# Hybrid encoder block: v column first over eight banks, both halves of the output projection in one bank, first left operands formed earlier

## Chip, core and metric

The kernel runs on one core of one Trainium2 chip. The metric is the device time of one execution in microseconds. PE is the matrix engine, DVE the vector engine, ACT the scalar engine, POOL the general engine, SP the engine that issues most DMAs.

## The reference

x has 2048 rows of 1024. One input projection to 5 x 512 columns gives q, k, v (8 heads of 64) and u, vg (gated group). Attention is stick-breaking and strictly causal; the gated part mixes positions in blocks of 128. Both are normalized, concatenated and projected back; then follows an MLP with squared ReLU (1024 to 4096 to 1024) and a last norm.

```python
    h = rmsnorm(x, norm_mix_g)
    q, k, v, u, vg = split(h @ w_in)
    a_out = stick_breaking_attention(q, k, v)
    b_out = gelu(u) * (W_s layernorm(gelu(vg)) + b_s)      # per block of 128 rows
    a_out = rmsnorm(a_out, out_norm_g[:512]); b_out = rmsnorm(b_out, out_norm_g[512:])
    x = x + concat(a_out, b_out) @ w_out
    x = x + square(relu(rmsnorm(x, norm_mlp_g) @ w_up)) @ w_down
    return rmsnorm(x, norm_final_g)
```

## The kernel before

Everything is fp32. Each matmul operand is split into a high part (ACT copy, L81 or L84) and a low part (DVE subtraction, L82 or L85), and `mm3` (L89 to L91) makes three matmuls of them: high x high, high x low, low x high. A bank of PSUM takes 512 columns.

The 2048 rows are four chunks of 512. The program runs in this order.

1. `proj([0, 1])`: input projection of chunks 0 and 1 together, five columns of 512. `weight` loads a quarter of a column into a staging tile `st` (three of them in all, shared with `operand`, which loads x transposed, and `norms`, which loads x for the row norms), splits it, and stores the halves to `wi_d` for chunks 2 and 3. `natural` makes 24 matmuls for one bank (a row block of 128 x 512 columns, both parts of eight k blocks), then calls the evacuation: `evac_vg` (gelu, LayerNorm), `evac_u` (gelu, and for each pair of row blocks the mixing matmuls at L244 and the product with u), `evac_v` (split and store). The order of columns is vg, u, k, q, v. `gelu` takes an ACT copy and square, a DVE scalar op (L213), a DVE product (L214), a sigmoid and a last product.
2. `proj([2])` and `proj([3])`, with the attention of earlier chunks between their matmuls. An attention step (`weigh`, `gather`) makes a score tile z for 128 queries and up to 512 keys on PE, a running product on DVE (the scans L331 and L334, the product L335), four transposes on PE (L345), a split of them (aT at L81 and L82) and two matmuls with v (L363, L364).
3. For each chunk an `Out`: `operands` loads a (attention, transposed) and b (gated), splits them and transposes b; `product` makes the output projection in groups of four row blocks: for each of two halves of 512 columns first b's part, then a's part, each in a bank of its own, each evacuated by one DVE operation at L509 that scales by the row norm and adds to x; `turn` norms the result and transposes it for the MLP. The first two Outs stand before `up_plain` (chunks 0 and 1), the third before `down_plain`, the fourth beside it.
4. `up_plain` and `down_plain` are the MLP of chunks 0 and 1 in the plain way, with attention beside them. `up_seven` and `down_seven` are the MLP of chunks 2 and 3 by a seven-product scheme: `Rights` forms sums of the activation tiles (`minus`, L668) and keeps seven of them split (`keep`), and each of 16 turns forms seven sums of weights (by POOL) and splits them (w0 to w6). All of `rest` stands within the first turn, after the last plain output.

`together` interleaves such generators at fixed ratios when the program is written; the building layer then sets the order on each engine. Tiles of 8 KB per partition (`t8`, 14 of them in one pool for Outs and plain MLP; the fourth Out has eight of its own) are handed on by slots: a load into a slot waits until its last reader is done. All loads except the stores to `wi_d` and some outputs are issued by SP, in order.

## Time and profile before

| | us |
|---|---|
| median of 3 runs (lowest, highest) | 2577.95 (2577.49, 2582.44) |
| the profiled execution | 2578.94 |
| its span on the core | 2577.2 |
| PE busy | 2435.4 |
| DVE busy | 1719.5 |
| ACT busy | 1154.8 |
| POOL busy | 321.3 |

The profiled execution is 1.0 above the median and has 1.7 outside its span. Matmuls overlap in their records, so start to start is their price, not their length. A wait names the instruction that was released and the one that released it. The windows give the mean granted clock of TensorE (1.00 is the upper of its levels of 2.4 and 1.2 GHz).

### The profile page before, as it was taken

The numbers are of one execution on the slowest core, as the hardware profiler recorded it, in microseconds if no ns is written. First come the engines' busy times: TensorE is split into PE (matmuls) and PEld (weight loads), VectorE is DVE, ScalarE is ACT, GpSimd is POOL, SyncE is SP. The second block draws the span as 40 slices with busy tenths as digits, with TensorE's granted clock in tenths as the row PEclk, the third lists the DMA queues.
The fourth block names the chain that finished last, engine by engine and source line by source line (L and its number), as shares of the span: only waits on it lengthen the run. The fifth ranks groups of instructions, "written<-read, shape, count | busy, mean of one in ns | idle before, by whom it ended". The sixth has DMA issues, their size and how long they took to land.

```text
span 2577.2 us, 30195 instructions
## 1 busy us (share of the span) xinstructions
PE 2435.4 (94%) x11328; PEld 1974.1 (77%) x11328; DVE 1719.5 (67%) x2312; ACT 1154.8 (45%) x2004; POOL 321.3 (12%) x263
## 2 busy tenths in 40 slices
PE   7799989998979999999989799999979999999997
PEld 5688767786757888888778688888767888778886
DVE  4733359877787666666676788744557665677787
ACT  5323236546454555555563544422135455433333
POOL 1100001101010000000010000010023222223331
PEclk9899999999989999999999999999999999999999
DMA  7378787678764344343355733255233434663422
GB/s 269 148 253 262 250 258 228 205 216 256 264 221 152 113 125 119 123 123 115 123 178 175 248 115 119 86 229 212 98 115 117 159 144 151 231 232 144 161 98 98
DMA packets 153714, 446.59 MB, mean 173 GB/s; under 512 B 12384, under 2 KB 28768, under 8 KB 134368
## 3 DMA queue, kind: packets, MB, share of 16 engines
q1 hardware_dynamic: 145232, 417.39, 48.5%
q0 software_dynamic: 4032, 25.17, 2.4%
q10 hardware_dynamic: 4304, 2.10, 0.3%
q8 instruction: 90, 1.47, 0.2%
q14 instruction: 56, 0.46, 0.1%
HBM read 314.59 MB, written 130.02 MB: 173 GB/s over the span
## 4 chain that ended last, share of the span: by engine, by line
PE 76%; DVE 14%; DMA 4%; ACT 2%; issue 2%; POOL 1%; SPq 0%; DVEq 0%; POOLq 0%; ACTq 0%
PE mm L90 21%; PE mm L91 21%; PE mm L89 21%; PE tr L345 3%; PE av L363 2%; PE av L364 2%; DVE w L82 2%; PE z L321 2%; PE z L320 2%; DVE pr L334 2%; DVE pr L331 2%; DVE aT L82 1%; DVE b L332 1%; DMA w_in<-wi_d 1%; DVE t L82 1%
## 5 line engine op out<-in xcount | busy, mean ns | idle before, releaser
L91 PE MATMUL mm<-t,t 128*128 128x512 f32 x1280 | 501.4, 392 | 0.0
L90 PE MATMUL mm<-t,t 128*128 128x512 f32 x1280 | 500.8, 391 | 0.0
L89 PE MATMUL mm<-t,t 128*128 128x512 f32 x1280 | 497.4, 392 | 2.6 <-DVE t L639 2.5
L326 ACT ACTIVATE kk<-z 128x512 f32<-128x512 f32 (+2 forms) x320 | 171.2, 535 | 382.2 <-PE z L321 262.9
L334 DVE TENSOR_TENSOR_SCAN pr<-kk,pr,zeros 128x513 f32<-128x513 f32 x192 | 248.7, 1295 | 118.0 <-ACT kk L326 117.6
L89 PEld LDWEIGHTS mm<-t,t 128*128 128x128 f32 x1280 | 240.5, 188 | 53.9 <-DVE t L639 2.9
L91 PEld LDWEIGHTS mm<-t,t 128*128 128x128 f32 x1280 | 240.7, 188 | 51.5
L90 PEld LDWEIGHTS mm<-t,t 128*128 128x128 f32 x1280 | 240.5, 188 | 50.7 <-DVE t L82 0.4
L345 PE MATMUL tr<-ident,b 128*128 128x128 f32 x1088 | 185.3, 283 | 40.8 <-DVE aT L82 28.6
L82 DVE TENSOR_TENSOR aT<-tr,aT 128x512 fp32r<-128x512 f32 (+1 forms) x320 | 191.2, 599 | 32.7 <-ACT aT L81 32.4
L81 ACT ACTIVATE aT<-tr 128x512 fp32r<-128x512 f32 (+1 forms) x320 | 173.0, 542 | 81.9 <-PE tr L345 80.4
L345 PEld LDWEIGHTS tr<-ident,b 128*128 128x128 f32 x1088 | 133.8, 144 | 87.2 <-DVE aT L82 38.8
L90 PE MATMUL mm<-w,w 128*128 128x512 f32 x448 | 177.0, 395 | 10.4 <-DVE w L82 8.8
L91 PE MATMUL mm<-w,w 128*128 128x512 f32 x448 | 175.9, 393 | 0.0
L89 PE MATMUL mm<-w,w 128*128 128x512 f32 x448 | 172.8, 391 | 0.2 <-ACT w L81 0.2
L81 ACT ACTIVATE t<-t 128x1024 fp32r<-128x1024 f32 x104 | 105.5, 1064 | 147.4 <-DMA t<-in_w_down 73.1
L328 ACT ACTIVATE b<-z 128x512 f32<-128x512 f32 (+2 forms) x320 | 170.8, 534 | 1.0 <-PE tr L345 1.0
L82 DVE TENSOR_TENSOR w<-raw,w 128x512 fp32r<-128x512 f32 (+1 forms) x136 | 155.9, 1149 | 13.3 <-ACT w L81 12.8
L331 DVE TENSOR_TENSOR_SCAN pr<-kk,zeros 128x128 f32<-128x128 f32 (+3 forms) x128 | 107.8, 844 | 79.8 <-ACT kk L326 79.2
L81 ACT ACTIVATE w<-raw 128x512 fp32r<-128x512 f32 (+1 forms) x136 | 107.2, 800 | 113.0 <-PE mm L91 98.2
L363 PE MATMUL av<-aT,vt 128*128 128x512 f32 (+1 forms) x320 | 142.6, 446 | 8.0 <-DVE ao L373 4.4
L82 DVE TENSOR_TENSOR t<-t,t 128x1024 fp32r<-128x1024 f32 x104 | 124.5, 1218 | 26.9 <-PE mm L90 15.0
(200 smaller groups left out, 4786.1 us busy)
## 6 DMA issues: line engine op xcount, KB each, us to landing
w_in<-wi_d SPq DMA_DIRECT2D x40, 1024.0 KB, 7.7
kt<-k_d SPq DMA_DIRECT2D x160, 256.0 KB, 4.8
s_d<-acts SPq DMA_DIRECT2D x16, 1792.0 KB, 6.2
raw<-s_d SPq DMA_DIRECT2D x28, 1024.0 KB, 4.8
t<-wo_d SPq DMA_DIRECT2D x24, 1024.0 KB, 8.4
wi_d<-w_in POOLq DMA_DIRECT2D x20, 1024.0 KB, 9.9
vt<-v_d SPq DMA_DIRECT2D x80, 256.0 KB, 2.8
t<-in_w_up SPq DMA_DIRECT2D x16, 1024.0 KB, 7.7
```

Source lines behind the costliest of these rows:

```text
L81: nc.scalar.activation(hi, src, AF.Copy)
L82: nc.vector.tensor_tensor(lo, src, hi.bitcast(F32), ALU.subtract)
L89: nc.tensor.matmul(ps, lh, rh, start=first, stop=False, skip_group_check=more)
L90: nc.tensor.matmul(ps, lh, rl, start=False, stop=False, skip_group_check=more)
L91: nc.tensor.matmul(ps, ll, rh, start=False, stop=last, skip_group_check=more)
L320: nc.tensor.matmul(z[:, :Z], ql, kt[:, 0, :Z], start=True, stop=False)
L326: nc.scalar.activation(kk[:, :L], z[:, :L], AF.Sigmoid, scale=-QK_SCALE)
L328: nc.scalar.activation(b[:, :L], z[:, :L], AF.Sigmoid, scale=QK_SCALE)
L331: nc.vector.tensor_tensor_scan(pr[:, L - 1::-1], kk[:, L - 1::-1], zeros[:, :L], 1.0, ALU.mult, ALU.add)
L334: nc.vector.tensor_tensor_scan(pr[:, ::-1], kk[:, ::-1], zeros, carry[tb], ALU.mult, ALU.add)
L345: nc.tensor.transpose(tr[:, tb * P:(tb + 1) * P], bs[tb][:, j * P:(j + 1) * P], ident)
L363: nc.tensor.matmul(av[:, t0:], vt[:, j, :], aT[:, 0, t0:], start=first, stop=False)
```

## The change

1. Start. The first column of `proj([0, 1])` is v, by `first_col`: eight banks open at once, the quarters of k outside, so that each quarter of the weights and operands feeds 48 matmuls. Staging tiles are seven of their own. The norms come after all operands. The columns then go vg, u, k, q.
2. `gelu`: the square carries the constant, and one DVE operation takes the place of two.
3. `Out`: b is scaled (by its row norm over a's) before its transposes, so that both parts of a half run into one bank, and one evacuation does for both: 8 instead of 16 in an Out. The row norms of a and b, with their small matmul, move into `operands`. All four weight tiles of a half are wanted before its first bank ends.
4. The raw weights and the first sums come from one set of nine tiles; `Lefts` forms w0 and w4 of the first turn beside `down_plain`; hc[4] is kept after the last plain output instead of before. In `down_seven` the weights are loaded in tiles of 8 KB instead of 16, and y and acc lie in such tiles.

```diff
+        col0 = 2 if cs[0] == 0 else 4 if gated_first else 1
...
+        def first_col(col, evac):
+            ws = weights(col)
+            banks = [[places[ci].ps() if (ci, tb) != (0, 3) else places[1].ps() for tb in range(NTB)]
+                     for ci in range(2)]
+            for k2 in range(KD // 2):
+                for ci, (c, pl) in enumerate(zip(cs, places)):
+                    for tb in range(NTB):
+                        ts_ = slice(tb * P, (tb + 1) * P)
+                        w, h = ws[k2], hT[ci][k2]
+                        for j in range(2):
+                            mm3(banks[ci][tb], h[:, 0, j, ts_], h[:, 1, j, ts_], w[:, 0, j, :], w[:, 1, j, :],
+                                k2 == 0 and j == 0, k2 == KD // 2 - 1 and j == 1)
+                        if k2 == KD // 2 - 1:
+                            evac(pl, c * TC + tb * P, ci * NTB + tb, banks[ci][tb])
+                        yield
...
-            nc.scalar.activation(t, dst, AF.Square)
-            nc.vector.tensor_scalar(t, t, GELU_A, 1.0, ALU.mult, ALU.add)
-            nc.vector.tensor_tensor(t, t, dst, ALU.mult)
+            nc.scalar.activation(t, dst, AF.Square, scale=GELU_A ** 0.5)
+            nc.vector.scalar_tensor_tensor(t, t, 1.0, dst, ALU.add, ALU.mult)
...
             for k2 in range(KD // 2):
-                if c == 0:
-                    ready[col0].append(weight(col0, k2))
-                hT[i].append(operand(c, pl, k2))
-            norms(c, pl)
-        if cs[0] == 0:
+                ready[col0].append(weight(col0, k2))
+                for i, (c, pl) in enumerate(zip(cs, places)):
+                    hT[i].append(operand(c, pl, k2))
+            for c, pl in zip(cs, places):
+                norms(c, pl)
             gates_ready()
+            yield from first_col(col0, evac_v)
...
+            nc.gpsimd.tensor_tensor(rb, rb, root, ALU.mult)
+            self.ras = [ra[:, tb:tb + 1] for tb in range(NTB)]
+            yield
             bm = self.bm = rm.pair([4, TC])
             for tb in range(NTB):
...
+                nc.scalar.activation(st[:, tb, :], st[:, tb, :], AF.Copy, scale=rb[:, tb:tb + 1])
                 ps = rm.ps((P, 4, P))
...
-            yield from group(0, 1, self.bm, self.rbs)
...
-            yield from group(1, 0, self.am, ras)
+            for half in range(2):
+                ws = [self.weights(half, part) for part in range(2)]
...
+                    for part, m in ((0, self.am), (1, self.bm)):
+                        for e in range(4):
+                            mm3(ps, m[0][:, e, ts_], m[1][:, e, ts_], ws[part][0][:, e, :], ws[part][1][:, e, :],
+                                part == 0 and e == 0, part == 1 and e == 3)
...
+                    nc.vector.scalar_tensor_tensor(ys[tb][:, hs], ps, self.ras[tb], ys[tb][:, hs], ALU.mult, ALU.add)
...
-            self.keep(4, b11, bigs)
...
             if step == 0:
-                self.keep(5, self.t2, bigs)
-                self.keep(1, self.b21, bigs)
+                self.keep(4, self.b11)
+                self.keep(5, self.t2)
+                self.keep(1, self.b21)
...
-    bufs = dict(bigx=2, w8=5, big=5, raw8=2, acts=2, t2=3)
-    rm = Room(None, None, bufs, dict(bigx=hx, w8=hx))
-    rights = Rights(lambda *a: rm.get("bigx", *a), lambda *a: rm.get("w8", *a))
+    rm = Room(None, None, dict(w8=9, s12=1, t8=12, acts=2, t2=2), dict(w8=hx, s12=hx))
+    rights = Rights(rm)
+    ahead = Lefts(rm, 0)
     together(down)
```

How this moves instructions, at four places. First the loads that SP issues at the start. Before, x (for the norms) stands between the operands of the two chunks, and the weights of the second column behind all of it:

```order
L121 DMA st<-in_w_in 128x1024
L135 DMA st<-in_x_t 128x1024
L145 DMA st<-in_x 128x1024 x4
L135 DMA st<-in_x_t 128x1024 x4
L145 DMA st<-in_x 128x1024 x4
L121 DMA st<-in_w_in 128x1024 x8
```

and now, from the last quarter of the operands on; the five weight tiles behind the gates are the four of vg and the first of u:

```order
L124 DMA stx<-in_w_in 128x1024
L138 DMA stx<-in_x_t 128x1024 x2
L148 DMA stx<-in_x 128x1024 x8
L942 DMA ln_g_t<-in_ln_g 128x512
L943 DMA ln_b_t<-in_ln_b 128x512
L944 DMA sgw_t<-in_sgw 128x1024
L946 DMA sgb_t<-in_sgb 128x8
L947 DMA outg_t<-in_outg 128x8
L124 DMA stx<-in_w_in 128x1024 x5
L226 DMA v_d<-qkv_st 128x8x128
```

All operands now stand ahead of x, and the stores of v alternate with weight loads from here on.

Second, PE where the first mixing stands (L244 before, L263 now; hT and hTx are the operands of chunks 0 and 1). Before, right behind the vg column, with a few matmuls of u around it:

```order
L91 MATMUL mm<-w_in,hTx 128x512
L89 MATMUL mm<-w_in,hT 128x512 x2
L244 MATMUL mm<-vn,sgw_t 128x128 x4
L89 MATMUL mm<-w_in,hTx 128x512 x2
L244 MATMUL mm<-vnx,sgw_t 128x128 x6
L90 MATMUL mm<-w_in,hT 128x512
```

and now behind two whole banks of u:

```order
L89 MATMUL mm<-w_in,hT 128x512
L90 MATMUL mm<-w_in,hT 128x512
L91 MATMUL mm<-w_in,hT 128x512
L263 MATMUL mm<-vn,sgw_t 128x128 x8
L89 MATMUL mm<-w_in,hT 128x512
L90 MATMUL mm<-w_in,hT 128x512
```

The mixing moved behind 48 matmuls. Third, PE inside the second Out's product (in mm<-t8,t8 the first tile is of the weights, the second of a or b; z, tr and av are of attention). Before, where the last group's weights (t8_6632, t8_6633) take over from the one before, one score tile is issued:

```order
L90 MATMUL mm_6596<-t8_6492,t8_6082 128x512
L91 MATMUL mm_6596<-t8_6491,t8_6083 128x512
L320 MATMUL z_6615<-kt_6610,qt_6316 128x512
L321 MATMUL z_6615<-kt_6610,qt_6316 128x512
L345 MATMUL tr_6624<-ident_60,b_6438 128x128
L363 MATMUL av_6593<-aT_6555,vt_6314 128x384
L364 MATMUL av_6593<-aT_6555,vt_6314 128x384
L89 MATMUL mm_6636<-t8_6632,t8_6180 128x512
L90 MATMUL mm_6636<-t8_6633,t8_6180 128x512
```

and now, where the second half's weights begin (t8_6438 is their first tile), three banks are begun with that one tile, and attention goes on before the next tile (t8_6439) is used:

```order
L370 MATMUL tr_6756<-ident_60,b_6598 128x128
L89 MATMUL mm_6446<-t8_6438,t8_6035 128x512
L89 MATMUL mm_6513<-t8_6438,t8_6035 128x512
L89 MATMUL mm_6581<-t8_6438,t8_6035 128x512
L370 MATMUL tr_6756<-ident_60,b_6631 128x128
L388 MATMUL av_6510<-aT_6681,vt_6385 128x512
L389 MATMUL av_6510<-aT_6681,vt_6385 128x512
L345 MATMUL z_6788<-kt_6659,qt_6664 128x512
L346 MATMUL z_6788<-kt_6659,qt_6664 128x512
L348 LDWEIGHTS ident_b_65
```

Two score tiles, z_6788 and the next, stand between the first and the second weight tile of that half, and one (z_6746) just before. Counted over the order of PE, score tiles z issued up to a place are:

| place on PE | before | now |
|---|---|---|
| last input projection ends | 78 | 78 |
| first Out: product begins, ends | 92, 98 | 96, 98 |
| second Out: product begins, ends | 116, 121 | 120, 125 |
| up_plain begins | 128 | 129 |
| third Out: operands begin | 250 | 251 |
| third Out: product begins, ends | 260, 267 | 256, 268 |
| down_plain begins | 276 | 280 |

Last DVE at the start of the seven products, from the last plain output on (w_15029 to w_15032 are Rights' sums, big the kept halves, nf the last norm). Before:

```order
L73 TENSOR_SCALAR nf_m<-nf_ssq 128x1
L648 SCALAR_TENSOR_TENSOR t_12270<-t_12270,nf_r,gfin_t 128x1024
L82 TENSOR_TENSOR big<-w_15029,big 128x1024 x2
L82 TENSOR_TENSOR big<-w_15031,big 128x1024 x2
L668 TENSOR_TENSOR w_15031<-w_15031,w_15029 128x1024
L82 TENSOR_TENSOR w_15948<-raw_15943,w_15948 128x512
L82 TENSOR_TENSOR w_15948<-t_15945,w_15948 128x512
L668 TENSOR_TENSOR w_15031<-w_15031,w_15029 128x1024
L82 TENSOR_TENSOR big<-w_15030,big 128x1024 x2
L82 TENSOR_TENSOR w_15967<-t_15945,w_15967 128x512
```

and now (w_14886 to w_14890 are Rights' sums, the t tiles the kept halves, s_14909 and w_14907 the sums of weights):

```order
L73 TENSOR_SCALAR nf_m<-nf_ssq 128x1
L673 SCALAR_TENSOR_TENSOR t_12185<-t_12185,nf_r,gfin_t 128x1024
L82 TENSOR_TENSOR t_15821<-w_14886,t_15820 128x1024 x2
L82 TENSOR_TENSOR t_15827<-w_14887,t_15826 128x1024 x2
L82 TENSOR_TENSOR t_15833<-w_14889,t_15832 128x1024 x2
L693 TENSOR_TENSOR w_14889<-w_14889,w_14887 128x1024 x2
L82 TENSOR_TENSOR w_15841<-s_14909,w_15841 128x512
L82 TENSOR_TENSOR w_15841<-w_14907,w_15841 128x512
L82 TENSOR_TENSOR t_15848<-w_14888,t_15847 128x1024 x2
L82 TENSOR_TENSOR w_15853<-w_14907,w_15853 128x512 x2
```

A third pair of kept halves (t_15821, hc[4]) moved to the front of this piece, and w0 and w4 have left it.

## Rows read from the trace of the kernel before

**Rows 1.** The page: busy time of an engine (share of span), and the chain by engine.

```profile
PE 2435.4 (94%) x11328; PEld 1974.1 (77%) x11328; DVE 1719.5 (67%) x2312; ACT 1154.8 (45%) x2004; POOL 321.3 (12%) x263
...
PE 76%; DVE 14%; DMA 4%; ACT 2%; issue 2%; POOL 1%; SPq 0%; DVEq 0%; POOLq 0%; ACTq 0%
```

**Rows 2.** Windows: busy us of PE, PEld, DVE, ACT, POOL (count), clock, DMA share, GB/s.

```profile
17.00:27.00 10.00, 6.83 (x23) 5.39 (x24) 5.28 (x6) 4.07 (x6) 1.06 (x2) 0.83 0.96 335
66.00:79.40 13.40, 0.22 (x2) 0.11 (x1) 12.96 (x30) 3.54 (x6) 3.10 (x3) 0.59 0.00 0
177.00:221.00 44.00, 44.00 (x193) 35.84 (x192) 15.50 (x20) 9.26 (x12) 2.12 (x4) 1.00 0.73 238
221.00:265.10 44.10, 44.10 (x196) 36.35 (x195) 15.02 (x24) 16.11 (x27) 4.25 (x11) 1.00 1.01 338
```

**Rows 3.** PE's waits from 0 to 131 us: in total, times, longest.

```profile
PE mm L244 <- DVE vnx L231: 13.2, 1, 13.2
PE mm L89 <- ACT hT L84: 11.0, 2, 7.2
PE mm L244 <- DVE ln_m L73: 1.7, 1, 1.7
```

**Rows 4.** DVE's lines from 79.4 to 131.2 us: busy us, mean ns.

```profile
L214 DVE TENSOR_TENSOR gelu_t<-gelu_t,u 128x512 f32<-128x512 f32 x7 | 4.8, 689 | 0.2
L213 DVE TENSOR_SCALAR gelu_t<-gelu_t 128x512 f32<-128x512 f32 x8 | 3.4, 426 | 11.5 <-ACT gelu_t L212 11.5
```

**Rows 5.** Transfers from 0 to 60 us: GB/s in 40 slices of 1.5 us.

```profile
GB/s 0 173 382 276 370 395 401 448 415 407 421 433 372 230 366 437 366 178 421 410 399 341 205 249 229 197 262 254 142 265 254 232 317 287 249 202 205 341 38 0
```

**Rows 6.** Windows of the first two Outs, and behind the third.

```profile
613.60:654.00 40.40, 30.06 (x142) 21.28 (x141) 38.13 (x60) 30.08 (x64) 7.63 (x8) 0.83 0.83 261
654.00:702.00 48.00, 48.00 (x222) 39.59 (x221) 32.11 (x47) 15.87 (x31) 2.11 (x3) 1.00 0.75 279
721.00:756.00 35.00, 24.43 (x105) 17.51 (x104) 33.69 (x47) 23.82 (x47) 8.27 (x6) 0.76 0.75 270
1416.00:1452.00 36.00, 22.82 (x120) 15.59 (x119) 28.47 (x39) 22.84 (x43) 1.48 (x3) 0.91 0.93 303
```

**Rows 7.** DVE's lines from 654 to 721 us.

```profile
L334 DVE TENSOR_TENSOR_SCAN pr<-kk,pr,zeros 128x513 f32<-128x513 f32 x7 | 8.9, 1278 | 0.3 <-ACT kk L326 0.3
L509 DVE SCALAR_TENSOR_TENSOR t<-mm,ra_r,t 128x512 f32<-128x512 f32 x8 | 6.0, 749 | 10.6 <-PE mm L91 10.6
...
L82 DVE TENSOR_TENSOR aT<-tr,aT 128x512 fp32r<-128x512 f32 (+1 forms) x6 | 3.6, 604 | 0.0
```

**Rows 8.** The page's DMA issues: KB each, median us to landing.

```profile
t<-wo_d SPq DMA_DIRECT2D x24, 1024.0 KB, 8.4
```

**Rows 9.** PE's waits from 1334 to 1452 us.

```profile
PE z L320 <- DMA kt<-k_d: 5.3, 1, 5.3
```

**Rows 10.** Timeline of DVE from 1917.5 us: start, us, instruction.

```profile
1923.22 6.78 DVE L82 TENSOR_TENSOR big<-w,big 128x1024 fp32r<-128x1024 f32 x4
1929.92 1.21 DVE L668 TENSOR_TENSOR w<-w,w 128x1024 f32<-128x1024 f32 x1
...
1933.39 4.54 DVE L82 TENSOR_TENSOR big<-w,big 128x1024 fp32r<-128x1024 f32 x2
...
1940.27 6.82 DVE L82 TENSOR_TENSOR big<-w,big 128x1024 fp32r<-128x1024 f32 x4
```

**Rows 11.** Timeline of POOL in the same stretch.

```profile
1923.59 0.57 POOL L649 DMA_DIRECT2D out_y<-t  x1 [1.61 <-DVE t L648]
1924.19 1.38 POOL L714 TENSOR_TENSOR t<-raw 128x512 f32<-128x512 f32 x1
1925.64 2.13 POOL L720 TENSOR_TENSOR raw<-raw 128x512 f32<-128x512 f32 x1
```

**Rows 12.** The window from 1918 to 1957 us.

```profile
1918.00:1957.00 39.00, 24.02 (x86) 18.67 (x87) 34.55 (x34) 22.08 (x32) 17.47 (x13) 0.78 0.28 94
```

**Rows 13.** DMA issues from 1917 to 1935 us.

```profile
out_y<-t POOLq DMA_DIRECT2D x3, 512.0 KB, 5.4
```

232 lines of the change are left out of this document (119 added, 113 removed).

## Prediction

> **What bounds the kernel now.** I read the page's first part and its chain first [rows 1]: PE is busy 94% of the span and stands for 76% of the chain that ended last, DVE for 14%. So PE sets the end, and what can be won lies where PE waits. A stretch without waits gives its price: 193 matmuls of 512 columns in 44.00 us, 0.228 us each [rows 2]. By that price I looked for the places where PE does less, by windows and by its waits. There are three, and they are the places that the change touches.
>
> First, the start. Until 131 us PE waits for DVE's vnx 13.2 us in one piece, for the first operand halves (hT) 11.0 us in two pieces of which 7.2 is the wait for the very first, and 1.7 for the LayerNorm [rows 3]. The stretch of the long wait has 0.22 us of PE work and 12.96 of DVE in 13.4 us, at a granted clock of 0.59 [rows 2]: DVE is behind with the gated column, and PE falls to the lower of its two levels meanwhile. Second, the attention around each Out: in 613.60 to 654.00 and 721.00 to 756.00 DVE is full (38.13 of 40.40; 33.69 of 35.00) and PE has 30.06 and 24.43; inside the products it is the reverse (PE 48.00 of 48.00, DVE 32.11) [rows 6]. Third, the start of the seven-product up-projection, 1918 to 1957: PE 24.02, DVE 34.55 of 39.00, at a granted clock of 0.78 [rows 12].
>
> **Part 1: v first, seven staging tiles.** The five columns are 5 x 192 matmuls x 0.228 = 218.9 us. The mixing (64 matmuls of 128 columns) and 8 or 9 small ones are between a quarter of that price and all of it each: 4 to 16 us, and since such matmuls are a quarter as wide I take 8. Sum 227. The fifth column ends at 265.1 [rows 2], so 38 us are lost; three rows of waits hold 25.9 of it [rows 3], the lower clock and short waits are the rest. What stays: 7.2 us before the first operand, some 2 at the lower clock behind it (17 to 27 us has 0.83 [rows 2]). What goes: the 3.8 us second wait, since eight open banks give PE 48 matmuls, 10.9 us, on each weight and operand pair, where before one staging tile had to come free for each; and the 13.2 and 1.7 us, since the gated column now starts with all norms done, its DVE chain runs beside it bank by bank, and two u banks stand ahead of the first mixing.
>
> What comes late next is DVE and the weights. A gated bank's evacuation is one STT for 0.75, one product 0.69 [rows 4], statistics that read 512 elements too, two STTs 1.5 and some small ones, about 4 to 5.5 us, against 24 x 0.228 = 5.47 of PE: level, so little is queued at the end, and two u banks (10.9 us) hide it. The weights: before the last v matmul, at about 7.2 + 43.8 + 2 = 53 us, some 16 MB must have moved (12 tiles of 0.52 MB, 8 of x, 4 MB of stored halves, the gates, the first gated tile). The first 60 us of before, in forty slices, ran at 366 to 448 GB/s in most slices of the first 30 us, where loads were queued, and at 142 to 341 behind them [rows 5]: 16 MB takes 36 to 44 us at the first, up to 60 at about 270. So 0 to 7 us may be lost here; I take 2, nearer the queued rate, since seven staging tiles keep loads queued. The stage ends at 227 + 9 + 2 = 238 to 239: **26 us won**, 19 to 29 as bounds. I count 25, as the v stores now share SP with the u weights: eight of them alternate with weight loads, and each waits for its evacuation. Behind them stand the u weights only, which are wanted 44 us later.
>
> **Part 2: gelu.** One STT (0.75, as [rows 7]) for a scalar op and a product (0.43 and 0.69 [rows 4]): 0.37 us of DVE less, 32 times, 12 us. Where PE is the bound it is worth nothing; the 16 in chunks 2 and 3 lie beside attention, where PE waits now and then. Bounds 0 and 6, **2 taken**. ACT's work is the same.
>
> **Part 3: one bank for both halves.** Eight of the 16 evacuations of an Out go, 8 x 0.75 = 6 us of DVE [rows 7], but inside the product, where PE is the bound: nothing there. Four ACT copies and a POOL chain of small operations come in ahead of b's transposes, beside attention, in a stretch where DVE is the bound: nothing either, or up to 3 us per Out if the transposes come late. What matters is where attention steps stand, by the counts of the table above. A step costs DVE a scan 1.28, a product 0.69 and a subtraction 0.60, 2.57 us [rows 4, 7]; on PE four matmuls of 512 columns, 0.91, and four transposes between a quarter and a whole of that, 1.1 to 1.8, 1.4 taken. In the first two Outs 5 to 8 more steps (three stand around the half boundary) run without product work, and 4 to 7 fewer under it: 5 x 2.57 - 4 x 1.4 - 1.4 = 5.8, or 8 x 2.57 - 7 x 1.4 - 1.4 = 9.4 us lost, the last 1.4 being one step more done by the time of the up-projection. In the third Out 5 more run under the product, 2 fewer outside, and 4 more are done before the plain down-projection: 5 x 1.4 - 2 x 2.57 - 4 x 1.4 = -3.7. Together **4 lost**. The fourth Out lies beside down_plain, where PE has work: nothing. The weights of the second half, 4 MB, can be loaded only when slots come free; a weight tile lands after 8.4 us [rows 8], and the steps at the boundary, 3 x 2.57 = 7.7, cover about that. With both ends: 8 us won if the boundary and the moved steps cost nothing and the evacuations freed DVE for attention, 20 lost if the boundary is bare.
>
> **Part 4: the left operands beside the second product.** Now DVE needs ten 1024-wide subtractions between the last plain output and the first full set; they take 18.1 us with four subtractions of 512 and two differences between them, 6.78 for the first four, 1.7 each, and 1.21 for one by itself [rows 10]. After: w0, w4 and hc0 are done earlier, but keep(4) is moved behind the last output: its tiles lie in the memory of the plain product's pool. Twelve subtractions remain, and keep(5) and keep(1) in part wait until the last out_y store has landed; it is issued at 1923.59 [rows 11] and such stores land 5.4 us later [rows 13], which is 11 us behind PE's last plain matmul (1918). From there by DVE's order: ten more subtractions at 1.2 to 1.8, 12 to 18 us, one difference of two such pieces 2.4, five of 512 3.4, and the last two products of PE behind that: PE ends its first turn 33 to 39 us after the plain product, against 39 now (1918 to 1957 [rows 12]). **3 us won**, 0 to 6.
>
> The Trainium skill speaks against this part: "SBUF — State Buffer" (section on the ports) says that VectorE with two SBUF inputs and a GpSimd operation that reads SBUF take a shared port by turns, and the other waits whole. The trace agrees in kind: the four that took 1.7 us each lie over two POOL additions of 1.38 and 2.13 us [rows 10, 11]. By that rule one addition less in the tight stretch gives 1.4 us back there and takes it beside down_plain, where DVE has room; the sum would be lower by 1.
>
> **Sum.** 2578.94 (the profiled run; 2577.2 span and 1.7 outside) - 25 - 2 + 4 - 3 = 2552.9. The median of the runs is 1.0 under the profiled run: 2552 is the forecast, 2545 to 2560 its own range. The seven-product loops and their end are PE-bound before and after, with deeper prefetch of raw weights: 0, give or take 3.
>
> **The rivals.** (a) The moved steps cost nothing and DVE's saved 12 + 24 us reach the attention stretches: 2552 - 4 - 8 = 2540. For it: DVE is full there [rows 6]. Against: the savings lie in products. (b) The start is limited by transfer at 270 GB/s and the first two boundaries are half bare: 2552 + 5 + 2 x 6 = 2569. For it: rates of 142 to 341 from 35 us on [rows 5]. Against: those were times with three staging tiles. (c) Slower: the second half's weights, 4 MB, at the 303 GB/s that such a stretch reaches [rows 6] take 14 us, and SP issues in order: key tiles of attention queued behind them come late, as the one wait of 5.3 us shows that they can [rows 9]. Then neither PE nor DVE has work: 14 + 5 = 19 us, in the second Out, the fourth (eight slots) and, by its slots, the first: 2552 - 4 + 57 = 2605. It decides against the change when each costs over 10 us. Against: the scheduler put steps at the boundary, and the first Out has slots for part of the weights. (d) The change doesn't do what it says: the gated column still ends with DVE behind, PE waits for its mixing as now, and only the 3.8 us go: 2552 + 15 = 2567, inside (b)'s price.
>
> **Chances.** Forecast 0.50; (a) 0.13; (b) and (d) together 0.22; within 0.2% (5 us, about what a measurement of this kernel can tell from no change) 0.05; (c) 0.10. So faster 0.85, same 0.05, slower 0.10. The range 2541 to 2571 leaves out (c), most of the even case and the tail of (a).
>
> **What would show it.** PE's wait for vnx gone and the five columns done at 236 to 242 us; a wait for w_in at 50 to 60 us would be the weights. Windows of the first two Outs: product stretches of 44 to 47 us with DVE nearly idle, attention stretches longer by 6 to 9 us together. A wait of the product on a DMA t<-wo_d would be (c). First turn of up_seven 33 to 37 us long. The forecast is wrong if attention behind the projection slows (q now ends last, just ahead of its use) or if the boundaries show bare waits.

## The result, and the profile after

The changed kernel takes 2621.15 us (median of 4; 2620.27 to 2626.71), the kernel before, on the same chip, 2580.19 (2577.49 to 2583.14): a ratio of 1.0163, with an interval of 1.0143 to 1.0183. It is 41 us slower, where 26 us faster was forecast, and the time lies beyond the range. The profiled executions have spans of 2618.6 and 2577.2 us.

The page of the changed kernel, busy time by engine (to be read beside [rows 1]):

```profile
PE 2454.1 (94%) x11328; PEld 1985.7 (76%) x11328; DVE 1684.6 (64%) x2236; ACT 1158.5 (44%) x2020; POOL 315.4 (12%) x259
```

DVE does 35 us less, as the diff says. PE has the same 11328 matmuls but is busy 18.7 us longer: the mean granted clock of the execution is 0.972 instead of 0.979, and behind a wait matmuls start further apart (0.43 us behind the one that ends at 2292.49, elsewhere 0.23). The other 22.7 of the 41.4 us are idle time of PE. A share of 94% shows neither. So I cut both traces at the ends of PE's stages (first or last matmul of each, from the traces; us):

| stretch | before | after | difference | forecast |
|---|---|---|---|---|
| start to the end of the five columns | 265.1 | 252.5 | -12.6 | -25 |
| to the end of chunk 3's projection, beside attention | 348.6 | 357.5 | +8.9 | -2 |
| first two Outs, to up_plain | 211.9 | 226.6 | +14.7 | +6 to +9 |
| up_plain | 509.0 | 506.7 | -2.2 | 0 |
| third Out | 117.3 | 120.2 | +2.9 | -4 |
| down_plain with the fourth Out | 465.8 | 471.7 | +5.9 | 0 |
| up_seven (its first turn 39.1, then 38.4) | 327.5 | 327.5 | 0 | -3 |
| down_seven | 322.3 | 344.6 | +22.3 | 0 |
| behind PE's last matmul | 9.8 | 11.2 | +1.4 | 0 |

Half of what was lost lies in down_seven, a stage that the forecast set at nothing. I take four places in order of time.

**The start.** PE's waits from 0 to 131 us in the changed kernel (in total, times, longest; beside [rows 3]):

```profile
PE mm L89 <- ACT hT L84: 7.2, 1, 7.2
PE mm L89 <- ACT vn L231: 3.7, 1, 3.7
PE mm L90 <- DVE w_in L82: 2.8, 1, 2.8
PE mm L89 <- ACT w_in L81: 1.8, 1, 1.8
PE mm L89 <- DVE qkv_st L85: 0.8, 1, 0.8
```

The waits for vnx, ln_m and the second operand are gone, as forecast. New ones have come. Windows of it (busy us of PE, PEld, DVE, ACT, POOL, then clock, DMA share, GB/s):

```profile
0.00:60.00 60.00, 52.80 (x222) 43.38 (x223) 23.41 (x36) 30.26 (x43) 10.60 (x27) 1.00 0.97 379
53.00:64.00 11.00, 11.00 (x50) 9.01 (x48) 0.00 (x0) 0.42 (x1) 0.22 (x1) 1.00 1.00 356
64.00:83.00 19.00, 14.47 (x52) 11.19 (x51) 8.79 (x14) 8.86 (x13) 1.46 (x2) 0.82 1.03 341
105.00:123.00 18.00, 13.41 (x56) 10.58 (x55) 15.86 (x27) 10.48 (x15) 5.56 (x7) 0.91 0.60 225
```

The transfers are full from the first microseconds to 83 us; before, the mean of the 40 slices of the first 60 us was 289 [rows 5]. From 53 to 64 us DVE does nothing at all and ACT 0.42 us, although v's eight banks stand finished (v's last matmul starts at 53.03). ACT's timeline tells why (start, us, instruction, in brackets the idle time before it and what ended it):

```profile
63.58 0.69 ACT L84 ACTIVATE qkv_st<-mm,x_r 128x512 fp32r<-128x512 f32 x1 [12.98 <-DMA v_d<-qkv_st]
...
73.24 0.69 ACT L84 ACTIVATE qkv_st<-mm,x_r 128x512 fp32r<-128x512 f32 x1 [3.10 <-DMA v_d<-qkv_st]
73.83 0.68 ACT L231 ACTIVATE vn<-mm,x_r 128x512 f32<-128x512 f32 x1
```

v's evacuations have two buffers, qkv_st; the third waits 12.98 us until the first store of v has landed behind everything else that is queued. The gated column's first evacuation (73.83) stands behind v's in ACT's order, and PE waits for it.

**The Outs.** Windows of the first two in the changed kernel (attention stretch, product; twice), beside [rows 6]:

```profile
610.00:657.50 47.50, 32.69 (x158) 24.03 (x158) 42.49 (x64) 37.41 (x78) 7.94 (x8) 0.82 0.80 245
657.50:704.00 46.50, 46.50 (x206) 38.33 (x205) 21.46 (x34) 11.76 (x22) 1.12 (x2) 0.97 0.75 281
725.00:771.70 46.70, 31.65 (x138) 22.14 (x137) 38.99 (x54) 30.52 (x61) 8.08 (x7) 0.78 0.74 242
771.70:824.00 52.30, 50.95 (x240) 41.34 (x240) 23.38 (x35) 10.59 (x23) 1.12 (x2) 1.00 0.41 146
```

The stretch from the projection's end to the first product grew from 39.6 us (613.6 to 653.2; the window of [rows 6] ends 0.8 later) to 47.5. From the end of the first product to the start of the second it was 54.1 (701.1 to 755.3) and is 67.8 (704.0 to 771.7). The products themselves went from 47.9 to 46.5 and from 51.1 to 52.2: next to nothing is given back there. Behind the second product, up to up_plain, 19.2 us became 12.7: 6.5 of the 21 us lost up to there come back.

**First turn of up_seven** (beside [rows 12]):

```profile
1935.30:1973.70 38.40, 25.96 (x86) 18.73 (x86) 29.84 (x36) 22.41 (x32) 15.26 (x10) 0.82 0.23 83
```

DVE's work in it fell from 34.55 to 29.84 us, PE's time by 0.7 only.

**down_seven.** The first 40 us of it in the kernel before, then its start in the changed kernel in windows, and below them SP's issues (start, us) from 2250 us on:

```profile
2245.00:2285.00 40.00, 36.12 (x149) 28.40 (x148) 34.76 (x29) 13.45 (x15) 20.63 (x7) 0.96 0.91 357
```

```profile
2268.00:2278.00 10.00, 5.63 (x16) 4.16 (x15) 5.25 (x4) 0.00 (x0) 7.50 (x4) 0.68 0.66 239
2278.00:2288.00 10.00, 2.95 (x12) 2.03 (x11) 2.77 (x4) 0.00 (x0) 2.55 (x2) 0.84 1.02 409
2288.00:2298.00 10.00, 5.51 (x13) 4.03 (x14) 6.48 (x6) 7.57 (x8) 0.00 (x0) 0.50 0.31 129
```

```profile
2250.15 6.90 SPq L808 DMA_DIRECT2D t<-in_w_down  x3
2257.11 2.25 SPq L819 DMA_DIRECT2D t<-y_d  x1
2272.19 0.37 SPq L587 DMA_DIRECT2D s_d<-acts  x1
2272.64 2.99 SPq L819 DMA_DIRECT2D t<-y_d  x3
2275.68 2.13 SPq L857 DMA_DIRECT2D w<-s_d  x2
```

In the changed kernel PE has 14.1 us of work in these 30. The twelve t8 tiles hold six of the seven right operands until up_seven's last turn has formed its products, so the weights of w_down, the four tiles of y, and the operands of the first turns are all wanted in one stretch; and SP, in order, issues the four y loads ahead of w<-s_d. What waited for that, from 2263 to 2303:

```profile
ACT w L81 <- DMA w<-s_d: 23.8, 1, 23.8
...
PE mm L89 <- ACT w L81: 11.5, 1, 11.5
...
PE mm L90 <- DVE w L82: 4.4, 1, 4.4
```

Of the 22.3 us some 15 go here (counted by PE's matmuls, the 192nd of down_seven starts 15.3 us later than before) and 7 near the end of the loop, where PE waits 7.3 us in one piece for DVE's w.

### The profile page after: what moved, and what is told of

It reads as the page before. It is cut to its first block, busy times and chain, and to the rows that moved or that the text cites. A ratio compares the mean times of both kernels' runs of the same rounds, so it can differ in the third digit from the quotient of the medians.

```text
span 2618.6 us, 30138 instructions
## 1 busy us (share of the span) xinstructions
PE 2454.1 (94%) x11328; PEld 1985.7 (76%) x11328; DVE 1684.6 (64%) x2236; ACT 1158.5 (44%) x2020; POOL 315.4 (12%) x259
## 5 line engine op out<-in xcount | busy, mean ns | idle before, releaser
L359 DVE TENSOR_TENSOR_SCAN pr<-kk,pr,zeros 128x513 f32<-128x513 f32 x192 | 248.3, 1293 | 117.3 <-ACT kk L351 116.9
L81 ACT ACTIVATE w<-w 128x512 fp32r<-128x512 f32 (+1 forms) x150 | 121.1, 825 | 299.6 <-DMA w<-s_d 172.3
L82 DVE TENSOR_TENSOR w<-w,w 128x512 fp32r<-128x512 f32 (+1 forms) x150 | 176.5, 1191 | 88.7 <-ACT w L81 86.8
L90 PE MATMUL mm<-w,w 128*128 128x512 f32 x512 | 204.1, 399 | 17.3 <-DVE w L82 17.3
L89 PE MATMUL mm<-w,w 128*128 128x512 f32 x512 | 201.4, 396 | 12.4 <-ACT w L81 11.5
L91 PE MATMUL mm<-w,w 128*128 128x512 f32 x512 | 202.8, 396 | 0.0
L89 PE MATMUL mm<-t,w 128*128 128x512 f32 x384 | 154.0, 401 | 8.9 <-DVE acts L775 4.7
```

Source lines behind the costliest of these rows:

```text
L81: nc.scalar.activation(hi, src, AF.Copy)
L82: nc.vector.tensor_tensor(lo, src, hi.bitcast(F32), ALU.subtract)
L89: nc.tensor.matmul(ps, lh, rh, start=first, stop=False, skip_group_check=more)
L90: nc.tensor.matmul(ps, lh, rl, start=False, stop=False, skip_group_check=more)
L91: nc.tensor.matmul(ps, ll, rh, start=False, stop=last, skip_group_check=more)
L359: nc.vector.tensor_tensor_scan(pr[:, ::-1], kk[:, ::-1], zeros, carry[tb], ALU.mult, ALU.add)
```

## The experiments

Twelve kernels, each beside runs of the kernel before on the same chip. Columns: where the fifth column ends; the stretch from there to the end of chunk 3's projection; the first two Outs; down_seven (us, from the trace of each).

| kernel | median us | ratio (interval) | columns | projections | Outs | down_seven |
|---|---|---|---|---|---|---|
| before | 2580 | | 265.1 | 348.6 | 211.9 | 322.3 |
| after | 2621.15 | 1.0163 (1.0143 to 1.0183) | 252.5 | 357.5 | 226.6 | 344.6 |
| b_start | 2574.99 | 0.9974 (0.9964 to 0.9984) | 257.0 | 352.1 | 212.7 | 321.8 |
| b_out | 2599.74 | 1.0073 (1.0057 to 1.0090) | 265.6 | 349.4 | 228.6 | 321.6 |
| b_tail | 2607.32 | 1.0096 (1.0077 to 1.0115) | 265.5 | 353.6 | 211.4 | 345.5 |
| b_gelu | 2580.47 | 0.9998 (0.9988 to 1.0009) | 264.6 | 353.6 | 211.3 | 320.1 |
| b_sg | 2574.13 | 0.9974 (0.9962 to 0.9987) | 253.3 | 358.6 | 209.9 | 321.9 |
| a_qy | 2615.72 | 1.0133 (1.0118 to 1.0149) | 255.3 | 357.2 | 227.3 | 337.4 |
| b_start_nov | 2559.58 | 0.9919 (0.9904 to 0.9935) | 247.5 | 350.2 | 210.7 | 318.8 |
| b_nov_g0w6 | 2559.77 | 0.9926 (0.9906 to 0.9946) | 247.3 | 356.8 | 209.8 | 321.7 |
| b_nov_pair | 2561.36 | 0.9926 (0.9910 to 0.9943) | 250.7 | 349.8 | 210.6 | 318.4 |
| b_out_nodep | 2591.06 | 1.0037 (1.0017 to 1.0057) | 266.0 | 350.8 | 215.7 | 318.3 |
| b_tail_yt | 2597.19 | 1.0065 (1.0041 to 1.0089) | 265.0 | 350.4 | 211.2 | 337.1 |
| b_tail_own | 2585.95 | 1.0024 (1.0010 to 1.0037) | 265.1 | 352.9 | 210.8 | 326.4 |

**The parts alone.** b_start takes over the hunks of proj (v first, the staging tiles) but for the merged gelu:

```diff
-        col0 = 4 if gated_first else 1
+        col0 = 2 if cs[0] == 0 else 4 if gated_first else 1
+            yield from first_col(col0, evac_v)
```

> The kernel before with the start alone: v first over eight banks and seven staging tiles; gelu, Out and the seven-product part as before. In the changed kernel the fifth column ended at 252.5 us instead of 265.1, and the projections of chunks 2 and 3 then gave back 9 us up to their end (610.0 against 613.6). Theory (two buffers: the stores of v take 14 us to land while loads keep the transfers full, and the third evacuation of v waits for a qkv_st tile): the fifth column ends at 252 to 254 again and PE loses 14 us between 64 and 125 us. If the 9 us given back come from the start (q last, loads of chunk 2 elsewhere), the chunk 3 projection ends at 608 to 611 and the whole is 0 to 4 us faster than before; if they come from gelu, it ends at 600 to 602 and the whole is 11 to 13 us faster.

b_out takes over Out.operands and Out.product:

```diff
-            yield from group(0, 1, self.bm, self.rbs)
+            for half in range(2):
+                ws = [self.weights(half, part) for part in range(2)]
```

> The kernel before with the new Out alone. Theory (attention steps that stood under the product now run without it, where DVE is full): the first two Outs take 222 to 228 us against 212, the third 119 to 122 against 117, the fourth 5 to 7 us more; the whole 20 to 26 us slower. Rival (the Outs lose only since the start moved loads and attention against them): within 6 us of before.

b_tail takes over Rights, Lefts, up_seven, down_seven and their tiles:

```diff
-    bufs = dict(bigx=2, w8=5, big=5, raw8=2, acts=2, t2=3)
+    rm = Room(None, None, dict(w8=9, s12=1, t8=12, acts=2, t2=2), dict(w8=hx, s12=hx))
```

> The kernel before with the changed seven-product part alone (Lefts, Rights, shared tiles, down_seven's loads). Theory (the y loads stand on SP ahead of the second turn's operand and behind the last store of acts; two shared tiles are held by raw weights in the last group): the first turn of up_seven 37 to 39 us as before (39.1), 11 to 16 us lost at the start of down_seven, some 7 near its end, the whole 20 to 24 us slower. Rival (these losses come from the moved phases of the other parts): down_seven as before, the whole within 4 us.

Measured: -5.8, +19 and +26.5 us, together +39.7 of the +41. The parts add up: parts 3 and 4 lose in their own stages (the table), and only the first one gains. Some of what was expected missed: b_start's columns end at 257.0, not at 252 to 254 (the rest came with the merged gelu, see b_sg), b_out's first two Outs take 228.6 us, just above 222 to 228, and its whole loses a little less than 20 to 26, and b_tail loses more than 20 to 24.

**a_qy: buffers or bytes at the start, and the order of y.** The whole change with three more buffers for v's evacuations, paid with two staging tiles, and the y loads moved behind the second and fourth operand load of down_seven:

```diff
-            st = sp.tile([P, NH, 2, HD], F32R, name="qkv_st", bufs=2)
+            if cs[0] == 0 and i % 5 < 3:
+                st = staging[0].tile([P, NH, 2, HD], F32R, name="v_st", bufs=3)
...
-            for t2 in range(2):
-                nc.sync.dma_start(y[t2], y_d[c][:, 2 * t2:2 * t2 + 2, :])
+                if g == 0 and n in (1, 3):
+                    cy = n // 2
...
+                    ys[cy] = [y[tb // 2][:, tb % 2, :] for tb in range(NTB)]
```

> The changed kernel with two repairs: five buffers for the evacuation of v in the first stage (three more, two staging tiles fewer), and in down_seven the y loads issued behind the second and fourth operand loads instead of ahead of the second. Theory: PE's losses between 64 and 125 us fall from 14 to under 4, the fifth column ends at 239 to 243 us (252.5 in the changed kernel); the wait of 11.5 us at the start of down_seven goes, 12 to 15 us won there; the wait of 7.3 near its end stays. The whole 20 to 28 us faster than the changed kernel, near 2595. Rival for the start (the transfers are full, not the buffers short): fifth column still at 249 to 254. Rival for the end (nine shared tiles are too few): the loss at its start stays over 8 us.

Two windows of a_qy, PE's waits from 95 to 140 us, and two rows of ACT's timeline:

```profile
64.00:83.00 19.00, 17.98 (x79) 14.51 (x78) 10.89 (x18) 7.87 (x11) 2.45 (x3) 1.00 1.03 319
98.00:138.00 40.00, 27.26 (x119) 22.03 (x118) 28.58 (x50) 16.96 (x27) 7.41 (x9) 0.83 0.44 171
```

```profile
PE mm L89 <- ACT w_in L81: 10.3, 1, 10.3
PE mm L90 <- DVE w_in L82: 2.5, 1, 2.5
```

```profile
89.10 0.72 ACT L84 ACTIVATE hT<-st,gmix_t 128x512 fp32r<-128x512 f32 x1 [10.68 <-DMA st<-in_x_t]
...
109.13 1.04 ACT L81 ACTIVATE w_in<-stx 128x1024 fp32r<-128x1024 f32 x1
```

The wait at 64 to 83 is gone, and the columns end at 255.3, not earlier: the loss moved to u. Its weights are split behind the gated evacuations in ACT's order (109.13), and these stood 10.68 us behind a load of chunk 2's operands. So more buffers for v, with two staging tiles fewer, only moved the wait; more buffers without that price weren't tried, so how much the lack of buffers costs by itself stays open. The y order is worth 7 us (344.6 to 337.4). The whole is 5 us faster than the changed kernel, where 20 to 28 were expected.

**b_start_nov: fewer bytes.** Part 1 without the store of v's split weights (4.2 MB); chunks 2 and 3 split v's weights again:

```diff
-            if cs[0] > 0:
+            if cs[0] > 0 and col != 2:
                 nc.sync.dma_start(w.bitcast(F32), wi_d[col, k2])
...
+            if col != 2:
                 nc.gpsimd.dma_start(wi_d[col, k2], w.bitcast(F32))
```

> The start alone (as b_start), without the 4.2 MB of stores of v's split weights; chunks 2 and 3 load and split v's weights themselves. In b_start the fifth column ended at 257.0 us, with the transfers full from 2 to 83 us. Theory (the transfers are the bound of the first 100 us, and which buffer waits follows from that): 4.2 MB at some 380 GB/s are 11 us, the fifth column ends at 244 to 249. Rival (buffers or DVE's chain, not bytes): it ends at 253 to 258. The eight splits added in chunks 2 and 3 cost 0 to 4 us later.

PE's waits from 52 to 131 us:

```profile
PE mm L89 <- ACT w_in L81: 3.7, 1, 3.7
PE mm L90 <- DVE w_in L82: 3.2, 1, 3.2
```

The columns end at 247.5 instead of 257.0, and the kernel is 15 us faster than part 1 with the store, 21 faster than before: with the next two, which are level with it, the best that ran. So bytes in the first 83 us are a cause of the first loss: the gated column's first evacuation starts at 64.87 us instead of 74.00 in b_start. It still stands behind v's in ACT's order, and one of those still waits 7.98 us for a store of v. Two waits for u's weights stay.

**b_nov_g0w6 and b_nov_pair: the rest of the start.** First a sixth buffer for split weights in the first stage (for one staging tile), with the merged gelu in that stage only:

```diff
+            if cs[0] == 0 and turn[0] % 6 == 0:
+                w = spx.tile([P, 2, 2, 512], F32R, name="w_inx", bufs=1)
```

> Part 1 without the store of v's split weights (as b_start_nov, 2559.6), the merged gelu in the first stage only, and a sixth buffer for split weights in the first stage in place of one of the seven staging tiles. Theory: the two waits for w_in between 97 and 130 us (3.7 and 3.2) come from having five buffers, so they go to under 3 together, the merge takes 2 to 4 more, and the fifth column ends at 240 to 243 us instead of 247.5; the projections behind it are untouched (348 to 353), the kernel is at 2552 to 2555. Rival: the waits are ACT's and DVE's splitting beside the v evacuations, a sixth buffer doesn't move them: 244 to 246 and 2556 to 2558.

Its window behind the gated column's last matmul, and two rows of ACT's timeline there:

```profile
98.00:110.00 12.00, 6.66 (x21) 4.80 (x21) 10.32 (x17) 7.35 (x10) 2.82 (x4) 0.77 0.22 63
```

```profile
101.98 1.04 ACT L81 ACTIVATE w_in<-stx 128x1024 fp32r<-128x1024 f32 x1
105.18 0.63 ACT L245 ACTIVATE gelu_t<-gelu_t 128x512 f32<-128x512 f32 x1 [2.16 <-DVE gelu_t L240]
```

Both expectations were too low: 247.3, unmoved. Two things cancel: the merge makes each gated bank 0.4 to 0.5 us shorter, and the first of them starts at 67.88 instead of 64.87, behind v's evacuations, one of which now waits 11.84 us for a store. DVE is full (10.32 of 12) with the last gated banks, about 5 us each with their waits for ACT and POOL, and u's third weight tile is split at 102 in ACT's order behind them; DVE's half of that split follows at 105. Transfers have a share of 0.22. So DVE's chain is behind at the end of the gated column after all. Then u two banks at a time, so that each weight tile gives PE twice the work:

```diff
-            yield from natural(3, evac_u)
+            yield from paired(3, evac_u) if cs[0] == 0 else natural(3, evac_u)
```

> As b_nov_g0w6 (part 1, no store of v's split weights, merged gelu in the first stage, six buffers for split weights), with u's column of the first stage computed two banks at a time, the weight tiles outermost, so that PE has 12 matmuls on a weight tile where it had 6. In b_nov_g0w6 the fifth column ends at 247.4: behind the gated column's last matmul (97.8) two tiles of u's weights are ready, and the third is split at 102 to 106 only, behind the last gated evacuations in ACT's and DVE's order; PE does 6.66 us of work in the 12 us from 98 to 110. Theory: the third tile comes when it came, and PE now has 24 matmuls, 5.5 us, for that time instead of 12, and 12 behind it, so 3 to 4 us are won: 243 to 245, whole kernel 2553 to 2558. Rival: u's evacuations now come in pairs, u's two buffers and the mixing behind them wait, and PE loses as much there: 246 to 249, 2558 to 2562.

The two windows of b_nov_pair from 98 us, and PE's longest wait in them:

```profile
98.00:110.00 12.00, 9.21 (x40) 7.01 (x39) 10.25 (x18) 6.89 (x10) 2.95 (x4) 1.00 0.16 39
110.00:131.00 21.00, 16.51 (x68) 13.07 (x67) 11.89 (x23) 4.65 (x8) 3.53 (x4) 0.84 0.74 303
```

```profile
PE mm L89 <- DVE vn L294: 3.7, 1, 3.7
```

PE gains 2.55 us where the theory said, and loses 4.5 behind it, where it waits 3.7 for the mixing's DVE step: the rival, a little beyond its numbers for the columns (250.7). The time stays at 0.9926 of before.

**The merged gelu: b_sg and b_gelu.** On top of part 1, and alone on the kernel before:

```diff
-            nc.scalar.activation(t, dst, AF.Square)
-            nc.vector.tensor_scalar(t, t, GELU_A, 1.0, ALU.mult, ALU.add)
-            nc.vector.tensor_tensor(t, t, dst, ALU.mult)
+            nc.scalar.activation(t, dst, AF.Square, scale=GELU_A ** 0.5)
+            nc.vector.scalar_tensor_tensor(t, t, 1.0, dst, ALU.add, ALU.mult)
```

> The start and the merged gelu operation, Out and the seven-product part as before. In the changed kernel the fifth column ended at 252.5 us against 257.0 in b_start, which has the old gelu. Theory (in the first stage DVE's chain of the gated columns is level with PE, so 0.37 us for each of 16 banks count there; beside attention they don't): the fifth column at 251 to 254, the whole 3 to 6 us faster than b_start. Rival (gelu's merged operation gives back beside attention what it gives in the first stage, as the 9 us that the changed kernel lost there might show): the whole equal to b_start within 2 us.

> The kernel before with the merged gelu step alone (one scalar_tensor_tensor and a scaled square instead of a scaled square, a tensor_scalar and a product). With part 1 in place the merge won 3.7 us of the five columns and the next two projections beside attention took 6 us more (358.6 against 352.1); the whole was level. Theory: the give-back belongs to the merge itself, so here too the columns end 2 to 4 us earlier than 265.1 and the stretch from there to the end of chunk 3's projection is 353 to 357 instead of 348.6; whole kernel within 3 us of before. Rival: the give-back came from the state that part 1 leaves behind (its late stores), so the stretch stays 347 to 351 and the kernel is 2 to 4 us faster.

With part 1 it won 3.7 us of the columns and the projections behind it took 6.5 more; alone it won 0.5 and they took 353.6 against 348.6. But the six kernels with the old gelu and without part 1 range from 348.6 to 353.6 there, and b_nov_g0w6, whose gelu there is the old one, has 356.8 (its trace is of the longest of its four executions, 6.8 us above their median). So the four kernels with the merge (353.6 to 358.6) are higher in the mean, by some 5 us, and the ranges overlap: whether the merge does it stays open. On the whole it is worth nothing: 0.9998.

**b_out_nodep: the dependence in Out.** Part 3 with b scaled by its own norm alone, so that its transposes and the first part of the bank don't need a's; the scale that a needs is left out, so the output isn't the reference's:

```diff
-            nc.gpsimd.tensor_tensor(rb, rb, root, ALU.mult)
...
-                    for part, m in ((0, self.am), (1, self.bm)):
+                    for part, m in ((1, self.bm), (0, self.am)):
```

> The new Out alone (as b_out), but b scaled by its own row norm only, without a's, so that its transposes and the first part of a bank (now b's) don't wait for the attention of the chunk; one bank, one evacuation and four tiles of weights at once as in b_out. The output is not the reference's: b's part lacks the factor of a's row norm. Theory (the new Out made b's transposes wait for a, so the first product matmul comes 10 to 15 us later, and attention steps fill that time alone): the first two Outs take 211 to 217 us (212 before, 228.6 in b_out), the third 116 to 118 (120.8 in b_out), the whole 2 us faster to 6 us slower than before. Rival (four weight tiles at once, or the place of the evacuations): 224 to 230, the whole still 15 to 20 us slower.

b_out loses 16.7 us in the first two Outs, this one 3.8: 13 of the 17 go with the dependence and the order that it forces (b now comes ahead of a in the loads, in the transposes and in a bank). PE's timeline in before, in the changed kernel and in b_out_nodep, the first transposes of b (mm<-ident,t) and the first row sums of a:

```profile
628.74 1.47 PE L462 MATMUL mm<-ident,t 128*128 128x128 f32 x12
...
664.51 0.95 PE L520 MATMUL mm<-ones,a_sq 128*128 128x1 f32 x8
```

```profile
637.30 0.95 PE L486 MATMUL mm<-ones,a_sq 128*128 128x1 f32 x8
...
641.03 0.66 PE L501 MATMUL mm<-ident,t 128*128 128x128 f32 x4 [1.45 <-ACT t L498]
```

```profile
638.27 1.12 PE L460 MATMUL mm<-ident,t 128*128 128x128 f32 x4 [0.89 <-ACT t L457]
...
653.84 1.51 PE L473 MATMUL mm<-ones,a_sq 128*128 128x1 f32 x8 [2.43 <-POOL a_sq L469]
```

Before, the transposes come 15.1 us behind the projection's end (613.6), and the row sums inside the product (664.5); now the row sums come first, and b's transposes stand 31 us behind the projection's end (610.0). In b_out_nodep b's transposes come first again, 21.5 us behind the projection's end (31.9 in b_out), and the row sums behind them, ahead of the product. Its first product begins 45.1 us behind the projection (39.6 before, 50.1 in b_out); from the end of the first to the start of the second it has 50.2 us (54.2 before, 69.2 in b_out): in the first Out half of the loss stays, in the second it is gone. The whole is 10 us slower than before, not 2 faster to 6 slower: the third Out takes 122.4 us against 117.3, and down_plain with the fourth 471.4 against 465.8. So the dependence does not explain what part 3 loses in the third and fourth Out, and that wasn't traced to one wait.

**b_tail_yt and b_tail_own: the end of down_seven.** b_tail with the y loads behind the operand loads, and in the first all w_down tiles taken from t8, so that none stands among the nine:

```diff
-                    st = self.rm.raw8([4, 512]) if g % 2 and h else self.rm.t8([4, 512])
+                    st = self.rm.t8([4, 512])
```

> The seven-product part alone (as b_tail, which lost 12.1 us in a wait at the start of down_seven and 10 near its end), with the y loads behind the second and fourth operand loads, and with no raw weights in the nine shared tiles (all of down_seven's raw weights in the tiles of 8 KB of the other set). Theory (order on SP at the start; too few shared tiles in the last group): down_seven takes 328 to 333 us against 345.5 in b_tail and 322.3 before; the wait of ACT for s_d in the last group falls from 35 us to under 10. Rival (DVE is the bound near the end): the loss of some 10 us near the end stays.

8 us came back (345.5 to 337.1, where 328 to 333 were expected), nearly all at the start: counted by PE's matmuls, b_tail is 14.7 us behind the kernel before at its 192nd and loses 10 more near the end; this one is 7.5 behind there and loses 10 near the end. Second, two of the nine tiles kept as the staging pair of the operands:

```diff
+        sts = [rm.raw8([4, TC]) for _ in range(2)]
...
-                st = rm.raw8([4, TC])
+                st = sts[turns[0] % 2]
```

> Part 4 alone (lefts ahead, nine tiles of 8 KB instead of five and two), with the y loads behind the first operand loads of down_seven, and with two of the nine tiles kept as the staging pair of down_seven's operands, which leaves seven to go round. In the shared nine a staging tile takes the place of an operand that PE read two turns ago, so its load starts only when PE has ended that turn, and ACT waits for w<-s_d. Theory: with a pair of its own a load waits for ACT's and DVE's split alone, as before; the wait of ACT for w<-s_d in the last 90 us goes from 35 (part 4 with y in its old place: 29) to under 5, PE's loss in the last 90 us from 14 to 6 to 8; down_seven takes 326 to 332 us (345.5 with part 4 as it is, 337.1 with y moved, 322.3 before), the kernel 2586 to 2592. Rival: DVE is behind there by its own work; the waits change their name and down_seven stays at 335 to 339, the kernel at 2595 to 2599.

ACT's waits in b_tail from 2500 to 2607, then in b_tail_own from 2480 to 2586:

```profile
ACT w L81 <- DMA w<-s_d: 34.4, 5, 12.4
```

```profile
ACT w L81 <- PE mm L91: 28.5, 9, 4.7
```

No wait for w<-s_d is left, and PE's for DVE's w fell from 12.1 to 2.8. down_seven takes 326.4 us, the kernel 2586. So the end was the tiles: in the shared nine a staging tile takes the place of an operand that PE reads until the turn before last ends, and its load starts there; a pair of its own comes free when ACT and DVE have split it. What is left of part 4 is 4 us in down_seven: 8 at its start, not traced further, of which 4 come back by the end. Against them stands 1 us won in up_seven, which kernels without part 4 show too (326.3 in b_gelu, 326.6 here).

## Why the prediction was wrong

**Part 1, the start: a third.** Alone it won 8.1 of the 25 us in the five columns (b_start); the rest of the 12.6 in the changed kernel came with the merged gelu. The wait for vnx went. The first column went as forecast: v's last matmul starts at 53.03 us, where 53 was said, so nothing of the "0 to 7 us" that "may be lost here" was lost. The step that failed is what was said of v's stores, "eight of them alternate with weight loads, and each waits for its evacuation", priced at 1 us. It had the wait one way only: the third evacuation waits 12.98 us for a store, and behind it in ACT's order stands the gated column, which ends at 104.7 us (96.8 in b_start_nov). The rate was right, 379 GB/s in the first 60 us, but I counted 16 MB up to the last v matmul, and at 377 GB/s some 20 had moved by then: the loads run ahead for the next columns, and the stores of split weights (8 of 1 MB) and of v share the rate. Fewer bytes give 9.5 us back (b_start_nov); more buffers, paid with staging tiles, none (a_qy). Also failed: "two u banks (10.9 us) hide it". u's weights are split behind the gated evacuations, so u could not run then (98 to 110 of b_nov_g0w6). That is rival (d) by its cause, DVE's chain, though PE waits for u's weights and not for its mixing. The sum of PE's work, 227, was about right: by the median start to start of each kind of matmul in b_nov_g0w6 it is 228, and its busy time of 234.8 in the six windows to 248 us holds matmuls at the lower clock besides.

**Part 2: the size is nil on the whole,** as its bound of 0 allowed: with part 1 the columns ended 3.7 us sooner (257.0 to 253.3), and the whole stayed at 0.9974.

**Part 3: the sign was right, the size was not,** +14.7 in the first two Outs against 5.8 to 9.4. Alone it cost 19 us, about its bad end of 20, but not by the bare boundary that this end stood for. The step that failed is "nothing either, or up to 3 us per Out if the transposes come late". I costed the ACT copies and the POOL chain by their durations, not by what they wait for: b's scale now needs a's norm, and a is what attention ends with. Of the 16 us by which b's first transposes moved, some 10 go when the dependence goes (31.9 us behind the projection's end in b_out, 21.5 in b_out_nodep). The count of score tiles also misled: they fell from 6 to 2 under the first product, but all of PE's instructions there from 222 [rows 6] to 206, so a product of 48.0 became 46.5 and no more, while the stretch ahead of it took the rest. In the third and fourth Out I had -3.7 and 0; they measured +2.9 and some +6, of which 3.3 is a wait of PE for a_sq; as b_out_nodep loses there too, the cause of these two stays open. Rival (c), which had the right sign at 2605, did not happen: no wait on t<-wo_d is among PE's waits in the Outs.

**Part 4: the order of DVE's work was right, the end was another engine's.** Of the 3 us forecast, 0.7 came (the range was 33 to 39, measured 38.4); the four other kernels with part 4 have 37.0 to 37.1, the nine without it 37.7 to 39.3, so at most 2 came. DVE fell to 29.84 of 38.4, but an operand of POOL came late: ACT waits for it, DVE behind ACT, and PE for what stands behind that in DVE's order. From 1935 to 1974:

```profile
ACT w L81 <- POOL w L754: 9.3, 2, 7.2
...
PE mm L89 <- DVE acts L775: 4.7, 1, 4.7
```

POOL's timeline in the changed kernel, a subtraction and an addition of the same shape:

```profile
1955.60 6.17 POOL L754 TENSOR_TENSOR w<-w,s 128x512 f32<-128x512 f32 x1 [13.75 <-DVE w L82]
1961.85 1.27 POOL L720 TENSOR_TENSOR s<-w 128x512 f32<-128x512 f32 x1
```

The first lies over four subtractions of DVE (1956.03 to 1960.65), the second over none of those, and takes a fifth of its time. The Trainium skill, "SBUF — State Buffer" (section "SBUF: two separate sides"), says that the two take one port pair by turns, each for a whole instruction. The trace agrees in kind, but here POOL stood back for four instructions of DVE in a row (4.62 us), and the one that waits can be POOL, where I had weighed the case that DVE waits.

**The loops "with deeper prefetch of raw weights: 0, give or take 3": the largest error,** 22 us. I read the tile counts (nine and twelve of 8 KB for seven of 16 and seven of 8) as more prefetch, and didn't ask when each comes free: the twelve are held by right operands until up_seven's last turn, and the staging pair became part of a ring that PE empties. Three experiments bear this out (a_qy, b_tail_yt, b_tail_own): y's order gives 7 to 8 back, a staging pair of its own 11 more, and w_down tiles outside the ring nothing of the 10 near the end. The 4 that are left stay open.

**What would show it** named the right views for the start and none for down_seven, since no term stood there. Its second condition for being wrong, bare boundaries, did not hold; the first, slower attention behind the projection, can't be told from the spread of that stretch.

## What to carry to other kernels

Where a change renames or regroups buffers, write down for each tile who frees it and when the next load into it is issued, before and after; as many bytes in one ring as in two cost 11 us here, and loads issued ahead of one that is wanted sooner 7 to 8 more. Where a scale is folded into another operand, look at what produces it: b's transposes now waited for a's norm. And in a stage whose transfers are full, count the stores and the loads that run ahead, not only what the stage needs, and ask which evacuation waits for a store.

## What the runs showed of the hardware

Two stores of 0.5 MB (v_d<-qkv_st), issued at 49.5 and 51.3 us behind a run of loads and beside the stores of split weights, took 14.6 us in the median to land, and x's loads 12.7 us in the first 60 us, where the same loads took 4.7 before. Full transfers alone don't make it so long: the other six such stores, issued from 65 to 84 us, up to 83 us at a DMA share of 1.03, landed in 4.5. Operations of POOL and DVE side by side slowed one or the other by more than I had allowed: 6.17 us for a POOL operation above, and DVE's timeline in the changed kernel has the same operation of 128x512 three times, two of them beside POOL operations of 128x1024 that last to 2270.96 us. The store behind them on SP, ahead of down_seven's second operand, is issued 9.2 us behind up_seven's end, 6.4 in the kernel before:

```profile
2266.00 2.77 DVE L584 TENSOR_TENSOR acts<-acts 128x512 f32<-128x512 f32 x1
2268.69 2.82 DVE L585 TENSOR_TENSOR acts<-acts 128x512 f32<-128x512 f32 x1
2271.44 0.68 DVE L586 TENSOR_TENSOR acts<-acts 128x512 f32<-128x512 f32 x1
```

And the clock adds to a wait: in the window from 2288 to 2298, in which the 11.5 us wait in down_seven ends (2292.49), it is granted at 0.50, the lower of its two levels, and 13 matmuls took 5.51 us.
